# A two-layer hybrid decoder trunk on one core: side-by-side first tiles, sums of squares on VectorE, attention scores from split operands, and the scale of each norm taken up two or more tiles later

## The chip, the cores and the metric

The kernel runs on 1 core of a Trainium2 chip. The metric is the device time of one execution in microseconds (us), median of the runs. TensorE (PE in the rows) does the matmuls, VectorE (DVE) and ScalarE (ACT) the elementwise work, GpSimd (POOL) some of it, and the DMA queue of SyncE (SP) brings the weights.

## The reference

Two layers over a sequence of 256 positions with 2048 channels, all in float32. Cut to what matters:

```python
for l in range(2):
    h = rms_norm(x, attn_norm_g[l])        # x * rsqrt(mean(x*x) + 1e-6) * g
    proj = h @ w_in[l]                     # 2048 -> 11026 columns, split into the branches
    p_a = silu(layer_norm(causal_conv31(a_val * sigmoid(a_gate)))) @ w_conv_out[l]   # 512 channels
    p_b = (rg_lru(causal_conv4(r_x)) * gelu(r_gate)) @ w_rnn_out[l]                 # 768 channels
    p_c = nsa_attention(...) @ w_attn_out[l]     # 6 query heads, 2 key/value heads of 128
    y = sigmoid(g_a) * p_a + sigmoid(g_b) * p_b + sigmoid(g_c) * p_c
    x = x + y @ w_o[l]
    h2 = rms_norm(x, mlp_norm_g[l])
    x = x + square(relu(h2 @ w_mlp_up[l])) @ w_mlp_down[l]     # 2048 -> 8192 -> 2048
return rms_norm(x, final_norm_g)
```

With 256 positions the two softmax branches of the attention beside the compressed one ("selected" and "window") both see every earlier position, so each has plain causal scores, q times k, one 256 by 256 matrix for each head and branch.

## The kernel before

Activations lie transposed, channels on the partitions, so a product of 2048 channels with a block of 128 output columns is one **unit**: 16 **pairs** of matmuls into one PSUM tile `pu` (`unit2`, line 211). Each float32 operand is split into a high part (rounded to the fast float32r format) and a low remainder. A pair is `wh` times the 512 columns of an `xhl` tile (256 high, 256 low), then `wl` times its 256 high columns; the two halves of `pu` are added when it is read out (`z`, lines 674 and 675). Weights come in halves of a unit, 8 blocks of 128 by 128: `wload` (line 186) loads `raw` by SP's queue, ScalarE rounds it to `wh`, VectorE subtracts to `wl`. `wnext` keeps three halves ahead (`AHEAD`), with four buffers for each of the three tiles. Each `xhl` tile is made by ScalarE (high) and VectorE (low) in `scaled`.

The opening (lines 631 to 638) queues two 512-column parts of the first half, four transfers of `x` (two tiles of 256 each, 256 KB), two parts of the second half, and the other four of `x`. The first unit then uses the tiles one after another.

The factor of a norm is not applied to `x` but to each unit's result, as `z * rb`. `squares` (line 308) forms the squares of the 16 tiles on ScalarE, and GpSimd adds 14 of them into `ssq[0]`; the last stays apart. In layer 0 all the squares follow the opening. `rsqrt_cols` (line 325) then runs four one-column float32 matmuls (two tiles, two halves of the sequence) that sum over the partitions, VectorE adds the epsilon, GpSimd takes the power -1/2, and two float32 matmuls spread the result over 128 partitions into `rb`. It is called after the first unit of each normed stage (lines 672 and 748), and every result waits for `rb`.

Beside the units run side tasks written as generators: the convolution branch (`conv_task`), the recurrent one (`rnn_task`), and the attention (`attn_task`). `pump` (line 257) lets a task take its next steps after a half or a unit when an estimate of the engines' time allows, and `finish` forces the rest before the unit that needs its result. The order on each engine is then set by Tile's scheduler from a model of time; `keep` pins an instruction to the order in which it is written.

In `conv_task` the layer norm over the 512 channels uses four float32 matmuls with `mean_w` and, for the squares, eight one-column ones. In `attn_task` (lines 584 to 628) each of 6 heads has two score tiles, one for each half of the queries: one float32 matmul of `qr` with `kr` for both branches (line 593; 2 by 128 or 2 by 256 columns), then one bfloat16 matmul that adds the causal mask in PSUM (line 594, `identb` and `causb`), then VectorE takes the row maximum. So there are 24 score tiles in the two layers, 12 of each size.

In the trace one float32 matmul stands as two records, so 8 records are 4 matmuls.

## Time and profile before

| | us |
|---|---|
| median of 3 runs | 2869.32 (2869.1 to 2869.8) |
| the profiled execution | 2869.82 |
| its span in the profile | 2867.7 |
| TensorE busy | 2845.9 (99%) |
| VectorE busy | 2078.6 (72%) |
| ScalarE busy | 1469.7 (51%) |
| GpSimd busy | 108.2 (4%) |

Busy time of TensorE counts matmuls that overlap in its pipeline, so its pace is read from the starts of successive matmuls. The profiled execution took 2.1 us more than its span, for what lies around it.

### The profile page before, as it was taken

How to read it: one execution, taken by the hardware profiler on the slowest of the kernel's cores; microseconds unless marked ns; L12 is line 12 of the kernel's file. 1: busy time of each engine (PE TensorE's matmuls, PEld its weight loads, DVE VectorE, ACT ScalarE, POOL GpSimd, SP SyncE). 2: the span in 40 equal slices, each digit the busy share in tenths (PEclk: the TensorE clock that was granted, in tenths of full speed). 3: DMA queues.
4: the chain of work that ended last, by engine and by line, in shares of the span. 5: the costliest groups of instructions: out<-in, count | busy, mean ns of one | idle time of the engine just before them, and what ended most of it. 6: DMA issues, size and time to landing. Idle time of an engine off the chain costs nothing.

```text
span 2867.7 us, 43143 instructions
## 1 busy us (share of the span) xinstructions
PE 2845.9 (99%) x16456; PEld 2496.3 (87%) x16456; DVE 2078.6 (72%) x3332; ACT 1469.7 (51%) x2249; POOL 108.2 (4%) x102
## 2 busy tenths in 40 slices
PE   8999999999999999999999999999999999999998
PEld 6888888888888888888888888888888888888888
DVE  7988877677676576665779788776776766756655
ACT  5448755555444344443544487555554444434444
POOL 2000000002000000000200000000020000000001
PEclk9999999999999999999999999999999999999999
DMA  6555654565555555555555556445555555555554
GB/s 216 191 184 171 205 171 153 188 195 190 187 189 190 191 191 191 190 189 189 190 187 190 178 184 212 155 158 186 195 190 188 190 189 189 190 190 191 193 190 148
DMA packets 153167, 534.29 MB, mean 186 GB/s; under 512 B 17280, under 2 KB 18176, under 8 KB 152960
## 3 DMA queue, kind: packets, MB, share of 16 engines
q1 hardware_dynamic: 151904, 529.15, 55.7%
q8 instruction: 129, 2.11, 0.3%
q0 software_dynamic: 768, 2.13, 0.3%
q14 instruction: 78, 0.64, 0.1%
q10 hardware_dynamic: 288, 0.26, 0.0%
HBM read 529.37 MB, written 2.10 MB: 185 GB/s over the span
## 4 chain that ended last, share of the span: by engine, by line
PE 98%; DMA 0%; ACT 0%; POOL 0%; DVE 0%; SPq 0%; issue 0%; POOLq 0%; DVEq 0%; ACTq 0%
PE pu L155 95%; PE pv L155 3%; POOL ssq L317 0%; PE pv L614 0%; DMA x<-in_xT_dram 0%; DMA raw<-in_win_dram 0%; ACT wh L151 0%; ACT sq L151 0%; DVE fin L132 0%; PE pv L575 0%; PE pv L493 0%; SPq L637 0%; SPq L193 0%; POOLq L934 0%; DVEq L934 0%
## 5 line engine op out<-in xcount | busy, mean ns | idle before, releaser
L151 ACT ACTIVATE wh<-raw 128x1024 fp32r<-128x1024 f32 (+2 forms) x1034 | 1067.6, 1033 | 1305.9 <-PE pu L155 698.7
L155 PE MATMUL pu<-xhl,wh 128*128 128x512 f32 x4800 | 1681.1, 393 | 9.6 <-DVE xhl L136 9.6
L132 DVE TENSOR_TENSOR wl<-raw,wh 128x1024 fp32r<-128x1024 f32 (+2 forms) x1034 | 1230.8, 1191 | 628.0 <-ACT wh L151 604.3
L155 PE MATMUL pu<-xhl,wl 128*128 128x256 f32 x4800 | 1348.6, 281 | 1.2 <-DVE wl L132 1.2
L155 PEld LDWEIGHTS pu<-xhl,wh 128*128 128x128 f32 x4800 | 899.8, 187 | 209.2 <-DVE xhl L136 10.0
L155 PEld LDWEIGHTS pu<-xhl,wl 128*128 128x128 f32 x4800 | 908.4, 189 | 5.3 <-DVE wl L132 1.8
L155 PE MATMUL pu<-ah,wh 128*128 128x512 f32 x2016 | 699.1, 391 | 0.0
L155 PE MATMUL pu<-ah,wl 128*128 128x256 f32 x2016 | 564.5, 280 | 0.0
L155 PEld LDWEIGHTS pu<-ah,wh 128*128 128x128 f32 x2016 | 377.0, 187 | 82.7
L155 PEld LDWEIGHTS pu<-ah,wl 128*128 128x128 f32 x2016 | 381.0, 189 | 0.0
L132 DVE TENSOR_TENSOR x<-x,pu 128x256 f32<-128x256 f32 x316 | 132.7, 421 | 87.9 <-PE pu L155 82.6
L155 PE MATMUL pu<-yhl,wh 128*128 128x512 f32 x512 | 177.5, 393 | 0.0
L317 POOL TENSOR_TENSOR ssq<-ssq,sq 128x256 f32<-128x256 f32 x69 | 91.1, 1320 | 2239.1 <-ACT sq L151 2238.1
L155 PE MATMUL pu<-yhl,wl 128*128 128x256 f32 x512 | 141.7, 277 | 0.0
L155 PEld LDWEIGHTS pu<-yhl,wh 128*128 128x128 f32 x512 | 95.8, 187 | 22.0
L132 DVE TENSOR_TENSOR z<-pu,z 128x256 f32<-128x256 f32 x268 | 111.1, 416 | 0.6 <-ACT z L151 0.6
L136 DVE SCALAR_TENSOR_TENSOR cacc<-u,hpar,cacc 128x255 f32<-128x255 f32 (+14 forms) x240 | 103.7, 461 | 0.0
L151 ACT ACTIVATE z<-pu 128x256 f32<-128x256 f32 x268 | 97.9, 368 | 0.0
L155 PEld LDWEIGHTS pu<-yhl,wl 128*128 128x128 f32 x512 | 96.2, 188 | 0.2
L155 PE MATMUL pu<-oh,wh 128*128 128x512 f32 x192 | 67.4, 391 | 0.0
L132 DVE TENSOR_TENSOR z<-z,rb 128x256 f32<-128x256 f32 x136 | 57.7, 424 | 5.1 <-ACT rb L151 0.8
L136 DVE SCALAR_TENSOR_TENSOR s<-z 128x256 f32<-128x256 f32 x128 | 54.3, 425 | 4.5
(284 smaller groups left out, 1681.7 us busy)
## 6 DMA issues: line engine op xcount, KB each, us to landing
raw<-in_win_dram SPq DMA_DIRECT2D x342, 512.0 KB, 3.3
raw<-in_wup_dram SPq DMA_DIRECT2D x256, 512.0 KB, 3.5
raw<-in_wdn_dram SPq DMA_DIRECT2D x256, 512.0 KB, 4.2
raw<-in_wo_dram SPq DMA_DIRECT2D x64, 512.0 KB, 4.3
raw<-in_wro_dram SPq DMA_DIRECT2D x32, 384.0 KB, 3.0
raw<-in_wao_dram SPq DMA_DIRECT2D x32, 384.0 KB, 3.2
raw<-in_wco_dram SPq DMA_DIRECT2D x32, 256.0 KB, 2.9
raw<-in_cw_dram SPq DMA_DIRECT2D x16, 512.0 KB, 4.2
```

Source lines behind the costliest of these rows:

```text
L132: return V.tensor_tensor(o, x, y, op=op)
L136: return V.scalar_tensor_tensor(o, x, s, y, op0=op0, op1=op1)
L151: return A.activation(o, x, f, scale=scale, **kw)
L155: return T.matmul(o, l, r, start=start, stop=stop)
L317: G.tensor_tensor(ssq[0], ssq[0], q, op=ALU.add)
```

## The change

Four parts, and what goes with them.

1. The opening. Transfers of `x` and 512-column weight parts now alternate, and the parts alternate between the first and second unit. The matmuls of these two units run in turn, four tiles of `x` at a time (`early`, `tile2`). Ahead of them, 12 bfloat16 matmuls on a constant tile `wz` run whose result nobody reads.
2. The norms. In layer 0 the squares are formed beside units 2 and 3 as eight tiles of 512 columns, and VectorE adds them (`sq0`); for the other norms GpSimd still adds 14 tiles, and VectorE adds the last one. `rsqrt_cols` is cut in two: `rsqrt_rows` and `spread`. Each is placed between the `wh` and the `wl` matmul of a given tile, pinned there: in layer 0 the sums in unit 5 and the spreading in unit 6, elsewhere in units 1 and 2. Results before that are kept (`late`, `waiting`) and finished in one go.
3. The layer norm in `conv_task`: VectorE adds the four channel blocks first, so that one matmul with `mean_w` and two one-column matmuls remain.
4. The scores: `qr` and `kr` are split into high and low, three float32r matmuls (high with high, high with low, low with high) take the place of the one in float32, and VectorE adds the mask in PSUM. `identb` and `causb` are gone.

```diff
+    def tile2(p, w, i, r, k, n, between=None):
+        h, lo = (v[:, i * 128:(i + 1) * 128] for v in w)
+        r1 = mm(p, h, r.rearrange("p a s -> p (a s)"), k == 0, False)
+        if between:
+            keep(r1)
+            between()
+        r2 = mm(p[:, :S], lo, r[:, 0, :], False, k == n - 1)
+        if between:
+            keep(r2)
...
-        if m in (0, KT - 1):
-            ssq[m] = q
+        if m == 0:
+            ssq[0] = q
+        elif m == KT - 1:
+            tt(ssq[0], ssq[0], q, ALU.add)
...
-        for m in range(4):
-            mm(p[:, :S], mean_w, at[m], m == 0, m == 3, 4)
+        tt(cs, acc[0], acc[1], ALU.add)
+        tt(cs[:, 0, :], cs[:, 0, :], cs[:, 1, :], ALU.add)
+        mm(p[:, :S], mean_w, cs[:, 0, :], True, True, 4)
...
-        _, rb = rsqrt_cols([sq[m // 2][:, m % 2, :] for m in range(4)], 512)
+        tt(sq[0], sq[0], sq[1], ALU.add)
+        tt(sq[0][:, 0, :], sq[0][:, 0, :], sq[0][:, 1, :], ALU.add)
+        _, rb = rsqrt_cols([sq[0][:, 0, :]], 512)
...
-                    mm(pb[:, :, :nk], q, kr[:, g, :, :nk], True, False, 4)
-                    mm(pb[:, :, t * 128:nk], identb, causb, False, True)
+                    mm(pb[:, :, :nk], qh, krh[:, g, :, :nk], True, False)
+                    mm(pb[:, :, :nk], qh, krl[g][:, :, :nk], False, False)
+                    mm(pb[:, :, :nk], ql, krh[:, g, :, :nk], False, True)
+                    tt(pb[:, :, t * 128:nk], pb[:, :, t * 128:nk],
+                       con[:, None, C_CAUS:C_CAUS + 128].to_broadcast([128, 2, 128]), ALU.add)
...
+    for _ in range(N_WARM):
+        T.matmul(pz, wz[:, :128], wz, start=True, stop=True)
...
+    for i in range(8):
+        nc.sync.dma_start(x[:, 2 * i:2 * i + 2, :], a["xT"][:, 2 * i:2 * i + 2, :])
+        xs += [scaled(k, gain[:, 0, k:k + 1]) for k in (2 * i, 2 * i + 1)]
+        u, c = i % 2, i // 2
+        if c % 2 == 0:
+            wt[u] = wtiles()
+        wpart(wt[u], first[u + 2 * (c // 2)], slice(c % 2 * 512, c % 2 * 512 + 512))
+        if u:
+            for v in range(2):
+                for k in range(4 * c, 4 * c + 4):
+                    tile2(early[v], wt[v][1:], k % 8, xs[k], k, KT)
...
+        first_norm, rb_at = l == 0, RB_AT if l == 0 else 2
+        norm = {rb_at - 1: {4: norm_sums}, rb_at: {2: norm_spread}}
...
+            if l == 0 and ui in (2, 3):
+                for i in range(4 * ui - 8, 4 * ui - 4):
+                    keep(act(sq0[i], x[:, 2 * i:2 * i + 2, :], AF.Square))
+                    if i:
+                        keep(tt(sq0[0], sq0[0], sq0[i], ALU.add))
+            late.append((nm, m, z))
+            if ui < rb_at:
+                continue
```

(`RB_AT` is 6, `N_WARM` 12.) How this moves instructions, at three places. On TensorE at the opening, before: all pairs write the first unit's tile `pu_178`.

```order
L155 MATMUL pu_178<-xhl_114,wh_105 128x512
L155 MATMUL pu_178<-xhl_114,wl_106 128x256
L155 MATMUL pu_178<-xhl_117,wh_105 128x512
L155 MATMUL pu_178<-xhl_117,wl_106 128x256
L155 MATMUL pu_178<-xhl_121,wh_105 128x512
L155 MATMUL pu_178<-xhl_121,wl_106 128x256
```

And now, behind the last of the twelve on `wz`: `pu_117` and `pu_118` are the tiles of the first and second unit, and the numbers on `xhl` tell the tiles of `x` apart.

```order
L680 MATMUL pv_102<-wz_100 128x512
L157 MATMUL pu_117<-xhl_120,wh_127 128x512
L157 MATMUL pu_117<-xhl_120,wl_128 128x256
L157 MATMUL pu_117<-xhl_123,wh_127 128x512
L157 MATMUL pu_117<-xhl_123,wl_128 128x256
L157 MATMUL pu_117<-xhl_133,wh_127 128x512
L157 MATMUL pu_117<-xhl_133,wl_128 128x256
L157 MATMUL pu_118<-xhl_120,wh_140 128x512
L157 MATMUL pu_117<-xhl_136,wh_127 128x512
L157 MATMUL pu_117<-xhl_136,wl_128 128x256
L157 MATMUL pu_118<-xhl_120,wl_141 128x256
```

Each tile of `x` is now used twice before the ninth pair asks for the fifth one. On TensorE at the norm of layer 0, before: the sums over `ssq` and `sq` stand in the fourth unit (`pu_391`), after 58 pairs.

```order
L155 MATMUL pu_391<-xhl_154,wh_366 128x512
L155 MATMUL pu_391<-xhl_154,wl_367 128x256
L155 MATMUL pv_271<-ones_84,ssq_225 128x1
L155 MATMUL pv_271<-ones_84,sq_269 128x1
L155 MATMUL pv_271<-ones_84,ssq_225 128x1
L155 MATMUL pv_271<-ones_84,sq_269 128x1
L155 MATMUL pu_391<-xhl_158,wh_366 128x512
```

Now: they stand between the two passes of the fifth tile of the sixth unit (`pu_462`), after 88 pairs, and the scheduler has put the first passes of the seventh (`pu_519`) ahead of them.

```order
L157 MATMUL pu_462<-xhl_162,wh_416 128x512
L157 MATMUL pu_519<-xhl_120,wh_464 128x512
L157 MATMUL pu_519<-xhl_120,wl_465 128x256
L157 MATMUL pu_519<-xhl_123,wh_464 128x512
L157 MATMUL pu_519<-xhl_123,wl_465 128x256
L157 MATMUL pu_519<-xhl_133,wh_464 128x512
L157 MATMUL pv_478<-ones_84,sq0_295 128x1 x4
L157 MATMUL pu_462<-xhl_162,wl_417 128x256
```

The spreading matmuls follow 11 pairs later, where before they followed 15 pairs after the sums. On VectorE at one score tile of 2 by 256 columns in layer 0, before: `nm` is the row maximum of the tile `pv_4327`.

```order
L132 TENSOR_TENSOR wl_4497<-raw_4495,wh_4496 128x1024
L597 TENSOR_REDUCE nm_4330<-pv_4327 128x2
L132 TENSOR_TENSOR wl_4532<-raw_4530,wh_4531 128x1024
L132 TENSOR_TENSOR el_4253<-pv_4248,eh_4252 128x384
L132 TENSOR_TENSOR z_4477<-pu_4412,z_4477 128x256
```

Now: the mask is added to the tile `pv_4815` in place, and the subtraction of a weight half and a result `z` stand between it and the maximum.

```order
L143 TENSOR_SCALAR e_4652<-e_4652,rg_4650 128x128 x2
L134 TENSOR_TENSOR pv_4815<-pv_4815,con_81 128x2x128
L134 TENSOR_TENSOR wl_4867<-raw_4865,wh_4866 128x768
L134 TENSOR_TENSOR z_4803<-pu_4755,z_4803 128x256
L641 TENSOR_REDUCE nm_4820<-pv_4815 128x2
```

In layer 0 TensorE's last matmul of the attention stood 191 pairs ahead of the first unit that uses its result, and now stands 43 ahead; in layer 1 it was 191 and is 73. Between the third score tile of 2 by 256 columns of the first head group and the first transposition of its weights there were 18 pairs in either layer, and there are now 24 in layer 0 and 25 in layer 1.

## Rows read from the trace of the kernel before

**Rows 1.** The page's first part: busy time of each engine, its share of the span, and the count of instructions; PE and PEld (weight loads) first.

```profile
PE 2845.9 (99%) x16456; PEld 2496.3 (87%) x16456; DVE 2078.6 (72%) x3332; ACT 1469.7 (51%) x2249; POOL 108.2 (4%) x102
```

**Rows 2.** The view of waits, for TensorE: who waited for whom, us in total, times, the longest.

```profile
PE pu L155 <- DVE xhl L136: 9.6, 2, 8.7
PE pv L155 <- POOL ssq L317: 3.3, 1, 3.3
```

**Rows 3.** The view of instruction groups with shapes kept apart, TensorE, in the stretch from 100 to 200 us: count, busy us, mean ns of one, idle time before.

```profile
L155 PE MATMUL pu<-xhl,wh 128*128 128x512 f32 x290 | 100.6, 391 | 0.0
```

**Rows 4.** The opening. First the timeline of TensorE (start us, duration us), then its groups in the stretch from 8.74 to 30.11 us, then the timeline of ScalarE and of VectorE.

```profile
8.75 0.80 PE L155 MATMUL pu<-xhl,wh 128*128 128x512 f32 x1 [8.75 <-DVE xhl L136]
...
L155 PE MATMUL pu<-xhl,wh 128*128 128x512 f32 x48 | 18.8, 428 | 9.6 <-DVE xhl L136 9.6
...
4.50 1.26 ACT L151 ACTIVATE wh<-raw 128x512 fp32r<-128x512 f32 x2 [2.27 <-DMA raw<-in_win_dram]
7.67 1.71 ACT L151 ACTIVATE xhl<-x,gain 128x256 fp32r<-128x256 f32 x4 [1.91 <-DMA x<-in_xT_dram]
10.09 1.70 ACT L151 ACTIVATE xhl<-x,gain 128x256 fp32r<-128x256 f32 x4 [0.72 <-DMA x<-in_xT_dram]
11.70 1.13 ACT L151 ACTIVATE wh<-raw 128x512 fp32r<-128x512 f32 x2
12.77 3.31 ACT L151 ACTIVATE xhl<-x,gain 128x256 fp32r<-128x256 f32 x8
...
12.35 1.29 DVE L132 TENSOR_TENSOR wl<-raw,wh 128x512 fp32r<-128x512 f32 x2
13.56 3.25 DVE L136 SCALAR_TENSOR_TENSOR xhl<-x,gain,xhl 128x256 fp32r<-128x256 f32 x8
```

**Rows 5.** The first norm of layer 0. The timeline of TensorE; then the busy time of each engine (with counts), the granted clock (PEclk), the DMA share and GB/s in the stretch from 35.70 to 42.53 us; then TensorE's groups in the stretch from 30.17 to 48.74 us; then the timeline of GpSimd.

```profile
33.47 0.28 PE L155 MATMUL pu<-xhl,wl 128*128 128x256 f32 x1
37.09 0.58 PE L155 MATMUL pv<-ones,ssq 128*128 128x1 f32 x2 [3.34 <-POOL ssq L317]
...
39.60 0.63 PE L155 MATMUL pu<-xhl,wh 128*128 128x512 f32 x1
...
40.24 0.63 PE L155 MATMUL pu<-xhl,wh 128*128 128x512 f32 x1
...
35.70:42.53 6.83, 5.45 (x19) 4.92 (x20) 1.08 (x3) 0.00 (x0) 4.30 (x3) 0.50 0.54 172
...
L155 PE MATMUL pu<-xhl,wh 128*128 128x512 f32 x32 | 13.0, 441 | 0.0
...
19.07 17.97 POOL L317 TENSOR_TENSOR ssq<-ssq,sq 128x256 f32<-128x256 f32 x14 [17.90 <-ACT sq L151]
39.23 0.72 POOL L334 TENSOR_TENSOR rc<-rc,half 128x2 f32<-128x2 f32 x1 [2.19 <-DVE rc L142]
```

**Rows 6.** The timeline of TensorE at the second norm of layer 0.

```profile
732.48 0.28 PE L155 MATMUL pv<-ones,ssq 128*128 128x1 f32 x2
...
733.07 0.48 PE L155 MATMUL pu<-xhl,wh 128*128 128x512 f32 x1
...
733.50 0.28 PE L155 MATMUL pv<-ones,sq 128*128 128x1 f32 x2
733.64 0.48 PE L155 MATMUL pu<-xhl,wh 128*128 128x512 f32 x1
```

**Rows 7.** The timeline of TensorE at the layer norm of the convolution branch, layer 0.

```profile
201.28 1.89 PE L155 MATMUL pv<-cacc,mean_w 128*128 128x256 f32 x8
202.82 0.58 PE L155 MATMUL pu<-xhl,wh 128*128 128x512 f32 x1
...
207.86 0.50 PE L155 MATMUL pv<-ones,csq 128*128 128x1 f32 x4
208.22 0.48 PE L155 MATMUL pu<-xhl,wh 128*128 128x512 f32 x1
...
212.47 1.39 PE L155 MATMUL pv<-ones,csq 128*128 128x1 f32 x12
213.73 0.48 PE L155 MATMUL pu<-xhl,wh 128*128 128x512 f32 x1
```

**Rows 8.** The timeline of TensorE at a score tile of 2 by 128 columns, and at one of 2 by 256.

```profile
406.74 0.59 PE L155 MATMUL pv<-kr,qr 128*128 128x256 f32 x2
...
407.37 0.44 PE L155 MATMUL pv<-pcT,vcn 45*128 45x384 f32 x1
...
457.34 0.40 PE L155 MATMUL pu<-xhl,wh 128*128 128x512 f32 x1
457.57 0.28 PE L155 MATMUL pu<-xhl,wl 128*128 128x256 f32 x1
457.69 1.02 PE L155 MATMUL pv<-kr,qr 128*128 128x512 f32 x2
...
458.57 0.48 PE L155 MATMUL pu<-xhl,wh 128*128 128x512 f32 x1
```

**Rows 9.** The timeline of VectorE in the attention stretch, and the busy time of each engine from 390 to 495 us (columns as in rows 5).

```profile
401.55 0.42 DVE L132 TENSOR_TENSOR z<-pu,z 128x256 f32<-128x256 f32 x1
...
415.89 1.23 DVE L132 TENSOR_TENSOR wl<-raw,wh 128x1024 fp32r<-128x1024 f32 x1 [1.50 <-ACT wh L151]
...
390.00:495.00 105.00, 105.00 (x599) 88.46 (x598) 79.36 (x182) 60.29 (x144) 0.00 (x0) 1.00 0.44 141
```

More of the change, by code (lines that the diff above doesn't have):

```diff
@@ L498, in attn_task @@
             yield
-        kr = cpool.tile([128, NKV, 2, S], F32, tag="kr", name="kr")
+        krh = cpool.tile([128, NKV, 2, S], F32R, tag="kr", name="krh")
+        krl = [hl(F32R, "krl") for _ in range(NKV)]
         for b, nm in enumerate(("ks", "kw")):
-            swap_rope(kv[nm], kr[:, :, b, :])
+            r = hl(name="krf")
+            swap_rope(kv[nm], r)
+            act(krh[:, :, b, :], r, AF.Copy)
+            for g in range(NKV):
+                tt(krl[g][:, b, :], r[:, g, :], f32(krh[:, g, b, :]), ALU.subtract)
             yield
@@ L504, in attn_task @@
         for i in range(3):
-            r = hl(name="qr")
+            r = hl(name="qrf")
             swap_rope(qn[i], r)
-            qr.append(r)
+            q = [hl(F32R, "qr") for _ in range(2)]
+            act(q[0], r, AF.Copy)
+            tt(q[1], r, f32(q[0]), ALU.subtract)
+            qr.append(q)
             yield
@@ L646, in trunk, with norm_sums, norm_spread @@
         ct = rt = at_ = None
+        av, late = {}, []
+        def norm_sums():
+            nonlocal rc
+            rc = rsqrt_rows([sq0[0][:, 0, :], sq0[0][:, 1, :]] if first_norm else [ssq[0]], D, pin=True)
+        def norm_spread():
+            nonlocal rb
+            rb = spread(rc, pin=True)
+        first_norm, rb_at = l == 0, RB_AT if l == 0 else 2
+        norm = {rb_at - 1: {4: norm_sums}, rb_at: {2: norm_spread}}
         def pair(d, key, m, name):
@@ L724, in trunk @@
                     y["s", m] = r
+        for ui, (nm, m) in enumerate(PLAN):
+            task = dict(pa=ct, pb=rt, pc=at_).get(nm)
+            if task is not None and m == 0:
+                finish(task)
+            if nm in ("kc1", "vc1"):
+                compress(l, nm == "vc1", m, kv[nm[:2]], cz)
+                pump()
+                continue
+            if l == 0 and ui < 2:
+                p = early[ui]
+            else:
+                p = big_ps()
+                unit2(p, dict(pa=ua, pb=rbt, pc=oh).get(nm, xs), norm.get(ui))
+            z = tmp("z")
+            act(z, p[:, S:], AF.Copy)
+            tt(z, p[:, :S], z, ALU.add)
+            if l == 0 and ui in (2, 3):
[5 more added lines that the diff above has]
+            if ui < rb_at:
+                continue
+            if l == 0 and ui == rb_at:
+                side.append(prepare())
+            while late:
+                evict(*late.pop(0))
             pump()
```

139 lines of the change are left out of this document (69 added, 70 removed).

## The prediction

> **What bounds the kernel now.** I read the page's first part, then the waits of TensorE, then its timeline wherever something other than the main product stands. TensorE is busy 99% of the span, VectorE 72% [rows 1]. Busy time counts overlapping matmuls twice, so the pace is read from a stretch of main product alone: 290 first passes in 100 us with no idle time before any [rows 3], about 0.346 us a pair and 5.54 a unit. There the engine cannot be helped by anything that the change does. What can be won is therefore of two kinds: time in which TensorE stands or runs at its lower clock, and matmuls beside the main product. The list of waits is short: 9.6 us for the first `xhl` tiles and 3.3 for the sum of squares in the first norm [rows 2]. No wait in the attention reaches the list, so the work of the other engines counts only where it would come late.
>
> **The opening.** The first matmul starts at 8.75, and the third unit's last pair is the 48th first pass before 30.11 [rows 4]. At the full pace 48 pairs take 16.6 us, so 13.5 us of those 30.1 are start and stumbles. Now the same transfers of 256 KB come in another order on the same queue. The first arrives when the first did (4.50), the third at 7.67 and the fifth at 10.09, when ScalarE could begin on them [rows 4]; from then on ScalarE and VectorE, not the transfers, set the feed, since ScalarE worked through eight tiles in a row. One round (two tiles of `x`, one 512-column part) costs ScalarE 2 x 0.41 + 0.57 = 1.39 us and VectorE 2 x 0.41 + 0.65 = 1.46 [rows 4]. Six rounds are left when the fifth transfer lands, VectorE half a microsecond behind ScalarE: 10.5 + 6 x 1.46 = 19.3 for the last `wl` part. TensorE has 32 pairs, 11.1 us, for the two units; it starts near 6 (4.5, two tiles, one part) and is then fed 8 pairs (2.8 us) in every two rounds (2.9 us), so it keeps up, and after 19.3 it has the four last pairs of the second unit to do: 20.7. The next `wl` half is there by 19.3 + 1.23 [rows 9]. The third unit then ends at 20.7 + 5.5 = 26.2 against 30.1: **3.9 us won**. The transfers of the constants now stand among the weight halves of units 2 and 3; the second half of unit 2 is needed only 8 pairs, 2.8 us, after the first, so I cost that at nothing; without that cover it is one transfer, 0.7 us at the pace at which ScalarE took a round's two. The squares beside units 2 and 3 replace those that ScalarE did at the same place before. Bounds: were TensorE alone the limit from about 8.5 on (third transfer and two tiles), its remaining 30 pairs would end at 18.9, 5.7 us won. The other end is the lower clock all the way, below. I take 3.9, the feed by VectorE, since its rows are of the same instructions.
>
> The twelve matmuls on `wz` depend on nothing that comes by DMA and are over, even at 0.43 us each (a 512-column pass at the lower clock, which is two thirds of the 0.64 us from 39.60 to 40.24 [rows 5]), 5.2 us after they start, about when the first tiles come. They cost nothing, and whatever they win is inside the term above.
>
> **The first norm.** After 33.47 TensorE waits 3.34 us for `ssq`, because 14 additions on GpSimd run from 19.07 to 37.04 [rows 5]. Afterwards the granted clock is 0.50, the 1.2 GHz level, from 35.70 to 42.53, and a pair takes 0.64 us [rows 5]. The two units with 32 first passes, from 30.11 to 48.74, take 18.63 us where 32 x 0.346 = 11.07 would do; 7.56 us too many [rows 5]. What remains now: eight records of sums and four of spreading. Eight took 0.59 + 0.14 = 0.73 at the full clock [rows 6], and four small ones 0.36 [rows 7]. So 7.56 - 1.1 = **6.5 us won**, if no new wait comes. The new places: the squares of units 2 and 3 are done when unit 4 ends, near 37.3, and the sums stand after 88 pairs, which is 20.7 + 56 x 0.346 = 40.1. The power on GpSimd took 0.72 us and ended 1.3 us or so after the last sum [rows 5]; the spreading stands 11 pairs, 3.8 us, behind the sums. A margin of more than 2 us at either place. Behind VectorE's step for the epsilon stand a `wl` half and results, and TensorE waits for these only three halves later (8 us).
>
> **The other norms** (three) have four records of sums instead of eight: 0.73 to 0.36, **1.1 us** together. VectorE's one addition more is off the path: it waits for a GpSimd addition that follows a square by a microsecond or two, while the sums stand 20 pairs (7 us) later.
>
> **The layer norm of the convolution**, twice: eight records with `mean_w` take 202.82 - 201.28 = 1.54 us, now two, 0.39; and sixteen one-column records take 1.26 + 0.36, now four, 0.36 [rows 7]. (1.15 + 1.26) x 2 = **4.8 us**. The four extra additions on VectorE are side work of a task whose result is used several units later.
>
> **The scores.** A tile of 2 by 256 columns takes 458.57 - 457.69 = 0.88 us, mask included; three float32r passes of 512 columns at 0.23 (457.34 to 457.57) make 0.69 [rows 8]. 12 x 0.19 = 2.3. A tile of 2 by 128 columns takes 0.63 to the next start with the mask matmul at its full share [rows 8], or 0.44 as half of the larger tile; three passes of 256 columns at 0.12 (457.57 to 457.69) make 0.36. I take 0.53, the middle: 12 x 0.17 = 2.1, bounds 1.0 and 3.2. Together **4.4 us**, 3.3 to 5.5. VectorE gets 24 mask additions, of 256 columns from PSUM, about 0.42 us each by the `z` additions [rows 9], and the splitting of `qr` and `kr`, in a stretch in which it is busy 79.36 of 105 us [rows 9]. The mask addition waits for the third score matmul; queued behind it are a `wl` part and a `z`, as before behind the maximum. The `wl` part is used at least one unit later. I cost this at nothing, with what it would cost below.
>
> **Sum.** 3.9 + 6.5 + 1.1 + 4.8 + 4.4 = 20.7 us. The span was 2867.7, so 2847.0, and 2849.1 with the 2.1 us around it; the profiled execution was 0.5 us above the median, so I predict **2848.6 us**.
>
> **Rivals.**
>
> (a) *The opening runs at the lower clock.* TensorE now starts with a few pairs and waits for the third transfer, and in this trace the clock was at its lower level after a wait of 3.34 us [rows 5]. If all 32 pairs took 0.64 us from 6.0 on, they would end at 26.5 and the third unit at 32.0, 1.9 us later than before, so 2848.6 + 5.8 = 2854.4. Against it: at the lower clock the same feed keeps TensorE busy without a gap (eight pairs 5.1 us, fed every 2.9), and it was in such a busy stretch that the clock rose before. I give 9%.
> The Trainium skill (TensorE: Matmul & The Clock Gate, section HAM oscillation — how this bites in real kernels) speaks against such an opening: short groups of matmuls parted by waits for DMA let the clock fall, and each group starts slow. The row at 35.70 agrees for one wait; no run here shows it yet for a chain of groups.
>
> (b) *A wait in place of the one removed.* The seven results kept in layer 0 are finished at once in unit 6, some 6 us of VectorE work beside 2.5 us of `wl` per unit; or the squares are late. If TensorE stands at the spreading or for a `wl` as long as it did before, with the lower clock after it, the 6.5 us are gone: 2855.1. Against it are the margins above and the three halves in hand. 9%.
>
> (c) *Slower: the attention.* The mask addition lengthens the chain of each score tile on VectorE, and an addition that comes behind a `wl` half costs 0.42 + 1.23 us [rows 9]. If TensorE stood that long at the transpositions of all 24 tiles, 39.6 us would be added: about 2888. It decides against the change from (20.7 + 5.7) / 24 = 1.1 us a tile. Against it: the order leaves 24 and 25 pairs (8.3 us) between the last score tile of a row of heads and the first transposition, where 18 (6.2 us) were enough for no wait. For it: in layer 0 the whole task now ends 43 pairs, 15 us, ahead of its user instead of 66 us. 4%; a part of it, up to a loss of 15 us, another 5% (2856 to 2864).
>
> (d) The forecast itself, 73%, with 2845.7 (scores 5.5, opening 5.7) to 2852 (scores 3.3, opening 1.5) as its own range.
>
> **How the numbers follow.** The likeliest case gives 2848.6. The range takes in the forecast's own bounds, (a) and (b): 2845.5 to 2856; what is left out is (c) in both forms, 9%, and the tails of the others. About 0.2% (5.7 us) is what a measurement of this kernel can tell from no change. Cases (a), (b), (d) and half of the partial (c) all lie below 2863.6: faster 0.92, same 0.04, slower 0.04.
>
> **What would show it.** In the profile after: the 48th first pass ends near 26 us; no wait for `ssq` or `sq0`, and full clock from there to the end; a busy time of TensorE lower by some 10 to 14 us; 0.36 us for the sums of the later norms; three passes with no gap at each score tile. A clock of 0.50 in the first 27 us is (a); an idle time of TensorE before the spreading matmul or a `wl` in units 6 to 9 is (b); waits for `e` at the transpositions are (c). The prediction is wrong if the sums on TensorE shrink as said and the time doesn't.

## The result, and the profile after

The changed kernel takes 2850.15 us (median of 4 runs, 2849.82 to 2852.05), the kernel before on the same chip 2869.21 (4 runs, 2868.08 to 2869.8): a ratio of 0.9935, 95% interval 0.9918 to 0.9953, 19.1 us. The profiled execution took 2849.82 with a span of 2848.1, where before it was 2867.7. The forecast was 2848.6.

The page of the changed kernel, busy time of each engine, then the windows view from the first record of the clock to the end of TensorE's work (busy time of the engines, granted clock 1.00, DMA share, GB/s):

```profile
PE 2836.5 (100%) x16420; PEld 2490.8 (87%) x16420; DVE 2095.5 (74%) x3388; ACT 1473.7 (52%) x2253; POOL 91.1 (3%) x88
...
6.47:2842.90 2836.43, 2831.49 (x16409) 2488.84 (x16407) 2092.19 (x3383) 1470.15 (x2247) 90.51 (x80) 1.00 0.57 188
```

TensorE is busy 9.4 us less than in [rows 1], a little below the 10 to 14 us that the prediction gave as a sign; the twelve matmuls on `wz` are 5.2 us of what is new in it. The other 10.2 us of the span's gain are time in which TensorE stood. (Time at the lower clock counts as busy.) The view of waits, TensorE:

```profile
PE pv L157 <- POOL rc L902: 2.1, 1, 2.1
PE pv L680 <- DVE wz L677: 1.5, 1, 1.5
PE pv L157 <- DVE sq L134: 0.7, 1, 0.7
PE pu L157 <- DVE xhl L138: 0.5, 1, 0.5
PE pu L157 <- ACT wh L153: 0.4, 1, 0.4
PE pu L157 <- DVE wl L134: 0.2, 1, 0.2
```

The 9.6 and 3.3 us of [rows 2] are gone. The wait for `rc` belongs to the last norm and stood at 2.1 before too. The one for `sq` is new, 0.7 us, and none lies in the attention.

Where the time went is read by counting: TensorE's first passes of pairs (the `wh` matmuls into `pu`) are numbered in the order of their starts, and the same number is looked up in both traces. At the full pace a pair takes 0.3467 us, so a stretch's length says at once what it holds beyond the main product.

| stretch | before, us | after, us | won | forecast |
|---|---|---|---|---|
| start to pair 49 (three units) | 30.12 | 25.89 | 4.2 | 3.9 |
| pairs 49 to 113 (first norm) | 29.72 | 24.70 | 5.0 | 6.5 |
| the other three norms (their excess) | 4.31 | 2.75 | 1.6 | 1.1 |
| pairs 481 to 1393 (branches, layer 0) | 367.92 | 363.76 | 4.2 | 9.2 for |
| pairs 4400 to 5329 (branches, layer 1) | 373.83 | 368.73 | 5.1 | both layers |
| behind the last pair (from the first matmul of the last block to the end) | 20.63 | 21.02 | -0.4 | 0 |

The rows add up to 19.7, the difference of the spans.

**Opening.** TensorE's groups from 6.19 to 25.88 us, then its timeline at its start and at the first place where it stood (start us, duration us; the bracket is idle time before), then VectorE's timeline:

```profile
L157 PE MATMUL pu<-xhl,wh 128*128 128x512 f32 x48 | 17.3, 407 | 0.9 <-DVE xhl L138 0.5 <-ACT wh L153 0.4
```

```profile
1.46 5.22 PE L680 MATMUL pv<-wz 128*128 128x512 bf16 x12 [1.46 <-DVE wz L677]
6.20 0.72 PE L157 MATMUL pu<-xhl,wh 128*128 128x512 f32 x1
...
8.18 0.74 PE L157 MATMUL pu<-xhl,wh 128*128 128x512 f32 x2 [0.45 <-ACT wh L153]
...
9.12 0.39 PE L157 MATMUL pu<-xhl,wh 128*128 128x512 f32 x1
...
9.47 0.40 PE L157 MATMUL pu<-xhl,wh 128*128 128x512 f32 x1
```

```profile
17.80 0.69 DVE L134 TENSOR_TENSOR wl<-raw,wh 128x512 fp32r<-128x512 f32 x1
```

The 48th first pass lies before 25.88 where [rows 4] have it before 30.11. The last `wl` part is done at 18.49; the forecast had 19.3. After a wait of 0.45 us the pairs start 0.35 us apart (9.12, 9.47), the full pace. The end of the third unit is not exact to the tenth: in the nine traced executions with this opening (the changed kernel and eight of the runs below) it lies between 25.27 and 26.19.

**First norm.** TensorE at the sums (the product of `ones` with `sq`), then VectorE and ScalarE ahead of them, then the windows view around them (busy time of the engines, granted clock 1.00):

```profile
40.55 1.02 PE L157 MATMUL pv<-ones,sq 128*128 128x1 f32 x8 [0.66 <-DVE sq L134]
41.44 0.36 PE L157 MATMUL pu<-xhl,wl 128*128 128x256 f32 x1
```

```profile
38.59 1.22 DVE L134 TENSOR_TENSOR wl<-raw,wh 128x1024 fp32r<-128x1024 f32 x1 [0.74 <-ACT wh L153]
39.73 0.68 DVE L134 TENSOR_TENSOR sq<-sq,sq 128x512 f32<-128x512 f32 x1
```

```profile
37.49 1.06 ACT L153 ACTIVATE wh<-raw 128x1024 fp32r<-128x1024 f32 x1 [1.51 <-PE pu L157]
```

```profile
37.06:50.58 13.52, 12.86 (x79) 11.23 (x78) 8.39 (x15) 5.06 (x7) 0.71 (x1) 1.00 0.51 175
```

The last addition of squares stands in VectorE's queue behind a `wl` part, this waits for ScalarE's `wh`, and that waited 1.51 us for TensorE to free the buffer. So the addition comes 0.66 us late, with nothing wrong with the squares themselves. The clock holds, which it did not in [rows 5].

**Layer norm, a later norm, a score tile** of 2 by 256 columns, all in TensorE's timeline:

```profile
203.70 0.59 PE L157 MATMUL pv<-cs,mean_w 128*128 128x256 f32 x2
203.94 0.47 PE L157 MATMUL pu<-xhl,wl 128*128 128x256 f32 x1
...
216.27 0.50 PE L157 MATMUL pv<-ones,csq 128*128 128x1 f32 x4
216.63 0.37 PE L157 MATMUL pu<-xhl,wl 128*128 128x256 f32 x1
...
450.12 0.40 PE L157 MATMUL pv<-krh,qr 128*128 128x512 f32 x1
450.36 0.40 PE L157 MATMUL pv<-krl,qr 128*128 128x512 f32 x1
450.59 0.40 PE L157 MATMUL pv<-krh,qr 128*128 128x512 f32 x1
450.82 0.39 PE L157 MATMUL pu<-rb__2761,wh 128*128 128x512 f32 x1
...
721.05 0.50 PE L157 MATMUL pv<-ones,ssq 128*128 128x1 f32 x4
721.41 0.36 PE L157 MATMUL pu<-xhl,wl 128*128 128x256 f32 x1
```

The product with `mean_w` takes 0.24 us (1.54 in [rows 7]), the sums of `csq` 0.36 (1.62), a later norm's sums 0.36 (0.73 in [rows 6]), the score tile 0.70 without a gap (0.88 in [rows 8]).

### The profile page after: what moved, and what is told of

Its sections match the earlier page's. It is cut to its first block, busy times and chain, and to the rows that moved or that the text cites. A ratio compares the mean times of both kernels' runs of the same rounds, so it can differ in the third digit from the quotient of the medians.

```text
span 2848.1 us, 43089 instructions
## 1 busy us (share of the span) xinstructions
PE 2836.5 (100%) x16420; PEld 2490.8 (87%) x16420; DVE 2095.5 (74%) x3388; ACT 1473.7 (52%) x2253; POOL 91.1 (3%) x88
## 4 chain that ended last, share of the span: by engine, by line
PE 99%; DMA 0%; DVE 0%; ACT 0%; SPq 0%; issue 0%; POOLq 0%; DVEq 0%; ACTq 0%
PE pu L157 96%; PE pv L157 3%; PE pv L658 0%; DMA x<-in_xT_dram 0%; DMA raw<-in_win_dram 0%; DVE fin L134 0%; ACT wh L153 0%; PE pv L616 0%; DVE wl L134 0%; PE pv L526 0%; ACT xhl L153 0%; SPq L194 0%; SPq L688 0%; POOLq L1023 0%; DVE sq L134 0%
## 5 line engine op out<-in xcount | busy, mean ns | idle before, releaser
L331 POOL TENSOR_TENSOR ssq<-ssq,sq 128x256 f32<-128x256 f32 x55 | 73.8, 1342 | 2175.3 <-ACT sq L153 2170.7
```

The lines of the kernel that those rows point to most:

```text
L331: G.tensor_tensor(ssq[0], ssq[0], q, op=ALU.add)
```

## The experiments

Each kernel is the changed one with one edit. A median is compared with the kernel before on the same chip, by its ratio; where a stretch is compared with the changed kernel, it is by the pair numbers above.

**A second pace.** One thing has to be known to read them. TensorE's groups from 100 to 200 us, first in the changed kernel, then in the one without the matmuls on `wz` (below):

```profile
L157 PE MATMUL pu<-xhl,wh 128*128 128x512 f32 x290 | 100.6, 391 | 0.0
```

```profile
L157 PE MATMUL pu<-xhl,wh 128*128 128x512 f32 x284 | 100.4, 399 | 0.0
```

The instructions are the same, the granted clock is 1.00 in both, and neither waits, yet one starts 290 pairs and the other 284: 0.3467 and 0.3535 us a pair. Such a state lasts for tens to hundreds of pairs (last section). In pairs 113 to 721 it is there in some runs and not in others whose instructions are the same. It is called the longer pace below. In a stretch of main product alone that the edit doesn't touch it is told apart by its place. In the branches it is counted over the pairs that have no other matmul and no wait in them or just ahead: what these take beyond 0.3467 us each is longer pace, and the rest is other matmuls and waits.

### The opening

*Without the matmuls on `wz`* (e1_nowarm).

```diff
-N_WARM, RB_AT = 12, 6
+N_WARM, RB_AT = 0, 6
```

> The changed kernel without the twelve matmuls on the constant tile. Theory A (the opening is fed by VectorE, so the clock in its first part hardly matters): the first pairs take 0.64 us instead of 0.35, eight or so of them before the clock rises, TensorE catches up with the feed, and the third unit ends at most 1 us later than in the changed kernel (25.9 us): span 2848.1 to 2849.1. Rival (short groups of matmuls parted by waits keep the clock at its lower level through the opening): 32 pairs at 0.64 us, third unit's end near 31 to 32, span 2853 to 2854.

Measured 2852.19 (2851.57 to 2853.47), ratio 0.9944 [0.9932, 0.9957], span 2850.4. TensorE's timeline at the start:

```profile
10.57 0.63 PE L157 MATMUL pu<-xhl,wh 128*128 128x512 f32 x1
...
11.21 0.63 PE L157 MATMUL pu<-xhl,wh 128*128 128x512 f32 x1
...
12.36 0.40 PE L157 MATMUL pu<-xhl,wh 128*128 128x512 f32 x1
...
12.71 0.40 PE L157 MATMUL pu<-xhl,wh 128*128 128x512 f32 x1
```

Until about 12 us the pairs start 0.64 apart, as at the lower clock of [rows 5], then 0.35. Still the third unit ends at 26.30, 0.4 later than in the changed kernel and 0.1 outside the 25.27 to 26.19 of the executions with the warm-up, so a price of the missing warm-up is hardly clear of their spread. The feed sets that end, not TensorE, as the prediction argued against rival (a). The rest of the span's difference is not the opening: pairs 49 to 113 are 1.0 shorter (no wait for `sq`), and pairs 113 to 721 ran at the longer pace, 2.9 more.

*The old order of transfers, units one after the other, `wz` kept* (e6_seq_open).

```diff
-    for i in range(8):
-        nc.sync.dma_start(x[:, 2 * i:2 * i + 2, :], a["xT"][:, 2 * i:2 * i + 2, :])
...
-        wpart(wt[u], first[u + 2 * (c // 2)], slice(c % 2 * 512, c % 2 * 512 + 512))
...
+    for i in range(4):
...
+            for j in range(2):
+                wpart(wt[u], first[2 * u], slice(j * 512, j * 512 + 512))
+        for j in (2 * i, 2 * i + 1):
+            nc.sync.dma_start(x[:, 2 * j:2 * j + 2, :], a["xT"][:, 2 * j:2 * j + 2, :])
...
+    for v in range(2):
...
+        for k in range(KT):
+            tile2(early[v], wt[k // 8][1:], k % 8, xs[k], k, KT)
```

> The changed kernel with the opening's order of before (first unit's first half, four transfers of x, its second half, the rest of x; the two units one after the other), with the twelve matmuls on the constant tile and all else as changed. Theory A (the interleaving is worth what the feed allows): first pair at 8.7 at the full clock, the first unit follows the tiles of x to about 17.5, the second waits for its weights, the third ends near 29.5 instead of 25.9: 3.6 us more, span about 2851.7. Rival (the squares that no longer stand beside the opening were the gain): the third unit ends near 27, span below 2849.5.

Measured 2851.49 (2850.85 to 2854.8), ratio 0.9941 [0.9928, 0.9955], span 2849.0. The first pair starts at 8.38 and the third unit ends at 28.09, 2.2 later. TensorE stood 1.9 us between the last `wz` matmul and the first pair, and the clock fell in spite of the warm-up. TensorE's timeline, and the windows view from 9.54 to 12.95 (granted clock 0.50):

```profile
8.38 0.50 PE L157 MATMUL pu<-xhl,wh 128*128 128x512 f32 x1 [1.87 <-DVE xhl L138]
```

```profile
9.54:12.95 3.41, 3.41 (x13) 2.73 (x11) 3.38 (x8) 3.41 (x9) 0.00 (x0) 0.50 1.06 405
```

Pairs 49 to 113 are 1.1 shorter (no wait for `sq`, and a better pace), so that only 1.0 is left at the end.

*All squares straight behind the opening, summed on VectorE* (e11_sq_open): the loop moves ahead of the three `wload`s behind the opening. This is not quite the place of before: there ScalarE formed two weight halves first (16.05 and 17.32 us) and the squares from 18.28, and GpSimd added them, while here VectorE has the additions too.

```diff
+    for i in range(8):
+        keep(act(sq0[i], x[:, 2 * i:2 * i + 2, :], AF.Square))
+        if i:
+            keep(tt(sq0[0], sq0[0], sq0[i], ALU.add))
...
-            if l == 0 and ui in (2, 3):
-                for i in range(4 * ui - 8, 4 * ui - 4):
-                    keep(act(sq0[i], x[:, 2 * i:2 * i + 2, :], AF.Square))
-                    if i:
-                        keep(tt(sq0[0], sq0[0], sq0[i], ALU.add))
```

> The changed kernel with all squares of the first norm formed directly behind the opening's tiles, ahead of the first weight half of unit 2 (about where they stood before the change), added by VectorE. Theory A (where the squares stood was a part of the 4.2 us won at the opening, since ScalarE and VectorE feed TensorE there): the weights of unit 2 come some 4 us later, TensorE waits about 3 us near 20 us, the third unit ends near 29 instead of 25.9, perhaps with a piece at the lower clock behind it, and no wait is left at the sums: span 2850.5 to 2852.5. Rival (the interleaving alone made the opening): span below 2849.

Measured 2855.02 (2854.33 to 2855.73), ratio 0.9952 [0.9938, 0.9965], span 2853.9. The third unit ends at 32.51, 6.6 us later, twice what was expected. TensorE's timeline, and the windows view from 22.91 to 29.74:

```profile
23.22 0.80 PE L157 MATMUL pu<-xhl,wh 128*128 128x512 f32 x1 [2.66 <-ACT wh L153]
```

```profile
22.91:29.74 6.83, 5.54 (x16) 4.36 (x17) 6.60 (x9) 3.63 (x6) 0.00 (x0) 0.50 0.45 137
```

`wh` comes late behind the squares, TensorE stands 2.66 us, and the clock is 0.50 for the next 6.8. So squares and their additions ahead of the weights of the third unit cost the opening more than the order of transfers (2.2). How much of that the kernel before paid is not shown, since its squares stood two weight halves later and its additions on GpSimd.

### The first norm

*The sums one unit earlier* (e4_rb5).

```diff
-N_WARM, RB_AT = 12, 6
+N_WARM, RB_AT = 12, 5
```

> The changed kernel with the sums of the first norm one unit earlier (RB_AT 5 for 6). In VectorE's order the four last additions of squares then stand together, with no weight part among them. Theory A (what is late at the sums is a place in VectorE's queue): the squares of unit 3 end 35 us from the start, the last addition near 35.8, the sums are reached near 33.9, so TensorE waits about 1.9 us instead of 0.7: span 2849.0 to 2849.6, clock at its full level or briefly below it. Rival (the additions are done when they are, at 40.5, and the place of the sums in TensorE's order decides): a wait of 6 us or more and the lower clock after it, span 2854 to 2857.

Measured 2855.08 (2853.57 to 2857.21), ratio 0.9955 [0.9941, 0.9968], span 2852.4. TensorE and VectorE:

```profile
37.53 1.02 PE L157 MATMUL pv<-ones,sq 128*128 128x1 f32 x8 [3.12 <-DVE sq L134]
```

```profile
30.35 3.71 DVE L134 TENSOR_TENSOR wl<-raw,wh 128x1024 fp32r<-128x1024 f32 x3
...
34.31 3.07 DVE L134 TENSOR_TENSOR sq<-sq,sq 128x512 f32<-128x512 f32 x4
```

A wait of 3.1 with the clock at 0.50 from 39.63 to 43.05; pairs 49 to 113 take 3.9 us more. The additions are late because three `wl` parts stand ahead of them. The wait was larger than the 1.9 expected and less than the rival's 6; the place in the queue decides it.

*The sums two units later* (e2_rb8).

```diff
-N_WARM, RB_AT = 12, 6
+N_WARM, RB_AT = 12, 8
```

> The changed kernel with the sums of the first norm two units later (RB_AT 8 for 6). Theory A (the 0.7 us for which TensorE still waits at these sums is the lateness of VectorE's last addition, which stands behind a weight part whose buffer TensorE itself frees late): the wait is gone, nothing else becomes late, span 2847.3 to 2847.6. Rival (nine results finished at once instead of seven make VectorE late with weight parts in units 8 to 11): TensorE waits there for 1 us or more, span 2848.5 or longer.

Measured 2858.86 (2855.21 to 2859.53), ratio 0.9964 [0.9951, 0.9976], span 2857.0. At the norm it is as expected: no wait for `sq`. Pairs 49 to 113 are 2.1 us shorter and pairs 113 to 481 1.5 longer, for the sums and the spreading (1.35) now stand behind pair 113; together 0.6 is won, about the wait. But the span is 8.9 us longer, and pairs 721 to 1633 alone account for 9.8. TensorE's timeline there, and the windows behind the waits:

```profile
436.95 0.55 PE L157 MATMUL pu<-xhl,wh 128*128 128x512 f32 x1 [1.73 <-DVE z L134]
...
553.94 0.51 PE L157 MATMUL pu<-oh,wh 128*128 128x512 f32 x1 [0.69 <-DVE oh L134]
...
559.31 0.50 PE L157 MATMUL pu<-oh,wh 128*128 128x512 f32 x1 [1.92 <-DVE z L134]
```

```profile
437.21:440.62 3.41, 3.41 (x12) 2.85 (x12) 3.38 (x13) 0.42 (x1) 0.00 (x0) 0.50 0.04 12
560.09:563.50 3.41, 3.41 (x13) 2.93 (x12) 3.41 (x9) 1.08 (x3) 0.00 (x0) 0.50 0.80 250
```

Results that are kept for longer let the side tasks begin later, and the attention of layer 0, which the prediction had 43 pairs ahead of its user, now ends behind it: `oh` is the attention's output, and TensorE waits for it at the product that uses it. The first of the three waits is at another place: at 436.95 TensorE waits for a result `z` that VectorE read out behind steps of the attention's compressed branch. So a delay made at 50 us is paid at 437 and, for the larger part, at 550.

*The squares earlier: six beside unit 2, two beside unit 3* (e10_sq62).

```diff
-                for i in range(4 * ui - 8, 4 * ui - 4):
+                for i in range(0, 6) if ui == 2 else range(6, 8):
```

> The changed kernel with six of the eight square tiles of the first norm formed beside unit 2 and two beside unit 3 (four and four in the changed one). In VectorE's order the last addition then stands one weight part further ahead. Theory A (the 0.7 us of wait at the sums is that place in VectorE's queue): the last addition ends near 38 us, TensorE reaches the sums at 39.8 and doesn't wait; span 2847.2 to 2847.6, everything else as it was. Rival (more squares beside unit 2 make the weights of unit 3 late): a wait at 26 us of 1 us or more, span 2848.5 or longer.

Measured 2851.65 (2848.79 to 2851.93, 5 runs), ratio 0.9936 [0.9922, 0.9949], span 2849.9. The wait for `sq` is gone, and pairs 49 to 113 are 0.85 shorter: that much the wait cost, with its surroundings. (The third unit ends at 25.62, inside the spread named above.) But pairs 113 to 721 ran at the longer pace in this execution (2.9 more). Two of its five runs lie at 2848.79 and 2849.54; it is not shown to beat the changed kernel.

### The layer norm and the scores

*The sums of the layer norm on TensorE again* (e5_ln_pe).

```diff
-        tt(cs, acc[0], acc[1], ALU.add)
-        tt(cs[:, 0, :], cs[:, 0, :], cs[:, 1, :], ALU.add)
-        mm(p[:, :S], mean_w, cs[:, 0, :], True, True, 4)
+        for m in range(4):
+            mm(p[:, :S], mean_w, at[m], m == 0, m == 3, 4)
...
-        _, rb = rsqrt_cols([sq[0][:, 0, :]], 512)
+        _, rb = rsqrt_cols([sq[m // 2][:, m % 2, :] for m in range(4)], 512)
```

> The changed kernel with the layer norm of the convolution summed on TensorE again (four float32 matmuls with the mean and eight one-column ones, in each layer). Theory A (what the change won there is the time of these matmuls and nothing else): 1.54 and 1.62 us a layer instead of 0.25 and 0.36, so 2 x 2.55 = 5.1 us more, span about 2853.0, give or take 1 us for the pace of the pairs (0.347 or 0.354 us). Rival (VectorE's four additions cost TensorE time elsewhere, so undoing them gives part back): less than 3.5 us more.

Measured 2855.79 (2855.58 to 2858.14), ratio 0.9957 [0.9942, 0.9972], span 2853.8. Pairs 481 to 1393 take 2.05 more and 4400 to 5329 2.14: 4.2 us, where the forecast's term was 4.8. But these stretches have 1.1 us less of the longer pace than in the changed kernel (2.9 against 4.0); the matmuls and what surrounds them are 5.3 more, which is what theory A expected for the groups alone (5.1). So VectorE's four additions cost TensorE nothing elsewhere. The other 1.6 of the span is longer pace in layer 1's second half.

*Scores in one float32 product, mask on VectorE* (e3_fp32_scores).

```diff
-                    mm(pb[:, :, :nk], qh, krh[:, g, :, :nk], True, False)
-                    mm(pb[:, :, :nk], qh, krl[g][:, :, :nk], False, False)
-                    mm(pb[:, :, :nk], ql, krh[:, g, :, :nk], False, True)
+                    mm(pb[:, :, :nk], q, kr[:, g, :, :nk], True, True, 4)
```

(Cut: `qr` and `kr` are no longer split into high and low.)

> The changed kernel with the scores as one float32 matmul of unsplit operands again, mask still added by VectorE. Theory A (the scores were won on TensorE alone): a tile of 2 by 256 columns goes from 0.69 back to about 0.86 us, one of 2 by 128 from 0.35 to 0.43 to 0.5, so 12 x 0.17 + 12 x 0.1 = 3.2 us more, span 2850.8 to 2852. Rival (the mask matmul was the larger part of what the scores won): less than 1.5 us more, span below 2849.6.

Measured 2852.14 (2851.94 to 2852.21), ratio 0.9943 [0.9931, 0.9956], span 2850.4. The two branch stretches take 0.7 and 1.4 more, 2.1 us. Here too 0.8 us less of it is longer pace (3.2 against 4.0), so the split by itself is worth 3.0.

This trace also shows a wait in the opening, which the edit doesn't touch, that left the clock at its full level; TensorE:

```profile
9.29 0.73 PE L157 MATMUL pu<-xhl,wh 128*128 128x512 f32 x2 [1.73 <-ACT wh L153]
...
10.24 0.39 PE L157 MATMUL pu<-xhl,wh 128*128 128x512 f32 x1
...
10.59 0.40 PE L157 MATMUL pu<-xhl,wh 128*128 128x512 f32 x1
```

*Split scores, mask on TensorE* (e7_mask_pe).

```diff
-                    tt(pb[:, :, t * 128:nk], pb[:, :, t * 128:nk],
-                       con[:, None, C_CAUS:C_CAUS + 128].to_broadcast([128, 2, 128]), ALU.add)
+                    mm(pb[:, :, t * 128:nk], identb, causb, False, True)
```

(Cut: `identb` and `causb` are made again, and the third score matmul no longer ends the sum.)

> The changed kernel with the causal mask added by TensorE again (the bfloat16 matmul on the identity), scores split as changed. Theory A (that matmul hides almost wholly behind its neighbours: with unsplit scores and VectorE's mask, layer 1's stretch of attention took 43.26 us beyond the main product, with TensorE's mask and unsplit scores 43.44): 24 x 0.01 to 0.04 us, span 2848.2 to 2849.2. Rival (it costs its 256 columns, 0.11 us each): 2.6 us more, span 2850.7.

Measured 2854.37 (2852.56 to 2855.86), ratio 0.9949 [0.9935, 0.9962], span 2854.1. TensorE's timeline at a tile:

```profile
450.65 0.28 PE L157 MATMUL pv<-causb,identb 128*128 128x256 bf16 x1
450.68 0.36 PE L157 MATMUL pu<-xhl,wl 128*128 128x256 f32 x1
450.89 0.40 PE L157 MATMUL pu<-xhl,wh 128*128 128x512 f32 x1
```

From the mask to the next `wh` are 0.24 us, where a `wl` pass alone takes 0.12: the mask costs 0.12 here, though the `wl` pass starts only 0.03 behind it. By stretches it is 1.58 in pairs 721 to 1393 and 1.47 in 4400 to 5329, 3.05 us for 24 tiles, and the longer pace is the same there to 0.1; the other 2.9 of the span is longer pace in pairs 113 to 721. The theory that the bfloat16 matmul hides behind its neighbours fell. It rested on the 0.02 between its start and the next in [rows 8], and the row behind those shows what that left out; the kernel before, TensorE:

```profile
458.89 0.28 PE L155 MATMUL pu<-xhl,wl 128*128 128x256 f32 x1
```

The `wh` pass behind the tile is followed after 0.32 us, not after 0.23: the mask's price stands in the pass behind it. Counted to the second start behind the group, less one pass of that kind, the 2 by 256 tile takes 0.975 us before, 0.857 with float32 and no mask (e3_fp32_scores), 0.691 in the changed kernel and 0.823 here. So the mask is 0.12 to 0.13 with either product, and the split 0.15 to 0.17.

### How much room the attention has

*The mask added twice, and four times, on VectorE* (e8_mask2, e8_mask4; the masked weights are the same).

```diff
+                    for _ in range(2):          (e8_mask4: range(4))
                         tt(pb[:, :, t * 128:nk], pb[:, :, t * 128:nk],
```

> The changed kernel with the mask added twice: 24 more additions of 0.42 us on VectorE. The attention ends 3 pairs ahead of its user in layer 0 (1389 against 1392) and 34 ahead in layer 1. Theory B (it costs nothing until its end passes its user): span 2847.5 to 2850, no wait in layer 1; in layer 0, where only a microsecond is in hand, a wait of up to 2 us at the first of those units. Rival (c): waits at the transpositions, 0.4 us or more for each tile, 10 us.

Measured 2852.16 (2851.57 to 2852.39), ratio 0.9941 [0.9928, 0.9955], span 2850.5. The attention's stretches stand within 0.1 of the changed kernel's; the 2.5 of span are longer pace in pairs 1633 to 4400 (1.6) and a later end (0.9).

> The changed kernel with the mask added four times on VectorE for every score tile (the sum beyond the first changes no weight, as masked scores are already at -1e30): 24 x 3 more additions of 256 columns, some 30 us of VectorE. In the order the attention then ends 25 pairs behind the start of the units that use it in layer 0 and 25 behind in layer 1 (1417 against 1392, 5353 against 5328). Theory B (the side chain costs TensorE nothing until its end passes its user, then it costs about what the run with RB_AT 8 lost there): some 5 to 10 us at units 87 to 102 in each layer, no waits before; span 2858 to 2868. Rival (c) of the prediction (TensorE stands at the transpositions of each tile): waits at all 24 tiles, 24 x 1 us or more. Third view (VectorE has room, so nothing happens): span 2847.5 to 2849.

Measured 2862.56 (2860.34 to 2864.83), ratio 0.9978 [0.9969, 0.9987], span 2861.7. TensorE's timeline in layer 0, and the window behind the last wait:

```profile
548.18 0.44 PE L157 MATMUL pv<-eh,vn 128*128 128x384 f32 x1 [0.36 <-ACT eh L153]
...
557.70 0.79 PE L157 MATMUL pu<-oh,wh 128*128 128x512 f32 x1 [1.93 <-DVE z L134]
```

```profile
557.72:561.13 3.41, 3.41 (x11) 2.93 (x12) 3.41 (x7) 1.10 (x3) 0.00 (x0) 0.50 0.70 186
```

Pairs 721 to 1633 take 5.8 more, and layer 1's branch and what follows it 6.3 (pairs 4400 to the last, 1.8 of it longer pace). The rest of the span's 13.6 is longer pace in pairs 1633 to 4400 (1.6). No tile waits, except for the very last `eh` and `el`; the loss is at the user of `oh`. So one mask addition a tile is free, one more is free, and three more cost some 12 us (10 without the longer pace). The place at which it decides is the end of the whole task, not the tile.

*The sums two units later, and the side tasks let in more readily* (e9_rb8_slack12).

```diff
-N_WARM, RB_AT = 12, 6
+N_WARM, RB_AT = 12, 8
...
-AHEAD, SLACK, PE_SIDE = 3, 1.4, 0.4
+AHEAD, SLACK, PE_SIDE = 3, 1.2, 0.4
```

`SLACK` multiplies the time that `pump` counts for a side step on VectorE and ScalarE.

> The sums of the first norm two units later (RB_AT 8) as in the run that lost 9 us, and the planner's allowance for side work cut from 1.4 to 1.2 (SLACK), so that the attention of layer 0 ends 132 pairs ahead of the first unit that uses it instead of 25 behind it. Theory A (that run lost its time because the side tasks, started two units later, reached the user of the attention too late): no wait at units 27 to 87, the wait of 0.7 us at the sums gone as well, span 2847.2 to 2848. Rival (nine results finished at once, or the sums' place, make VectorE late whatever the allowance): span 2853 or more.

Measured 2856.74 (2855.95 to 2857.64), ratio 0.9957 [0.9945, 0.997], span 2853.8. The attention's loss is gone (no wait at the user of `oh`, pairs 1393 to 1633 as in the changed kernel, 721 to 1633 within 0.1), which bears out that lateness was the cause in e2_rb8. But crowded side work now makes TensorE wait elsewhere, once where the results of units beside the convolution branch are read out:

```profile
279.98 0.47 PE L157 MATMUL pu<-xhl,wh 128*128 128x512 f32 x1 [1.89 <-DVE z L134]
```

Pairs 481 to 721 take 1.8 more and 4400 to 5329 3.5 more; 0.9 of the latter, and the 1.7 behind pair 5329, are longer pace.

## Why the prediction was right, step by step

The sum held: 20.7 us forecast, 19.6 found in the span, and each term has a measured counterpart of the kind that was forecast. That the sum came so near is in part luck: the layer norm and the scores won some 2 us more than their terms, and the longer pace, of which the prediction knew nothing, took about as much back.

- **Opening, 3.9: measured 4.2.** The reason was right: the feed by ScalarE and VectorE sets the end. But the new order of transfers is only half of it: undone alone it costs 2.2, and with the old order the third unit still ends 2.0 before the 30.1 of [rows 4]. What is left of the changed opening in that run is above all the warm-up and the squares, which stand further back and are added on VectorE. The prediction costed the squares at nothing, as the same work at the same place; that their place matters is shown by the run that put them behind the opening (6.6), but not how much of the 2.0 is theirs. The warm-up, costed inside the term, is worth about 0.4 by the one run without it, hardly more than the spread.
- **Rival (a)** did not come. With gaps of 0.45 and 0.50 us the pace stays at 0.35 a pair, and without the warm-up the pairs do start at the lower pace, but the feed hides most of it. The Trainium skill (TensorE: Matmul & The Clock Gate, section HAM oscillation — how this bites in real kernels) has short groups parted by waits each start slow. The changed kernel's opening does not show it; the run with the old order (1.9 us of standing) and the one with the squares at the opening (2.66) show the slow start behind one wait each, and the run with float32 scores shows full pace behind one of 1.73. None shows a chain of slow groups.
- **First norm, 6.5: measured 5.0.** This term was too large. The sums and the spreading were right in kind, and the clock held. But the prediction took the last square as the end of that chain and gave it more than 2 us of margin; it left out that the last addition has its place in VectorE's queue behind a `wl` part whose own input is late. That costs 0.66 of wait, 0.85 with its surroundings, by e10_sq62. The eight sum records took 0.89 from start to next start (40.55 to 41.44) where 0.73 was taken, and a part of the units ran at the longer pace (0.2). Rival (b) was the right mechanism at a tenth of its price.
- **Other norms, 1.1: measured 1.6.** Counted to the second start behind each group, the sums go from 0.89 to 0.45, 1.3 for the three; the forecast took 0.73 to 0.36 and left out the stretched passes. The last 0.2 is longer pace in the kernel before.
- **Layer norm 4.8 and scores 4.4, together 9.2: measured 9.3.** This agreement is luck. Without the longer pace the two branch stretches are 11.05 shorter than before; the longer pace costs 4.0 us in them now and cost 2.2 before, which leaves 9.3. Undone one at a time, and again without the longer pace, the terms are 5.3 for the layer norm, 3.0 for the split and 3.15 for the mask, 11.4 together. So the scores are worth 6.1, outside the 3.3 to 5.5 that the prediction gave them. The cause is the same in both terms: the groups of before were measured to the next start, which left out what the pass behind each group is stretched (0.09 us for a mask or one-column sums, 0.19 for `mean_w`). Counted to the second start, the layer norm's groups go from 1.73 to 0.43 and from 1.79 to 0.45 in each layer, 5.3 in all, and a 2 by 256 score tile from 0.975 to 0.691, where the forecast had 0.88 to 0.69. Whether the shorter groups themselves bring on the longer pace was not tested.
- **Costed at nothing:** the mask additions and the additions of the layer norm on VectorE. For the mask that held, with one whole addition a tile to spare; for the layer norm's additions too, since the run that undid them gave back the price of the matmuls and no more. **Rival (c)** gave the right lever and the wrong place: TensorE would not have stood at the transpositions of 24 tiles, but at the user of the attention, and the point from which it decides lies between 24 and 72 further additions a kernel, as the two runs show.

## What to carry to other kernels

A step that is moved on an in-order engine arrives when its queue lets it, so its lateness is counted from what stands ahead of it there, not from its own input. Side work that is given a later start cost little here until its last step passed its user, and then it cost far from where the edit was made, so look for the margin at the user. The price of a small group of matmuls is read to the second start behind it, since the pass that follows may be the one that pays.

## What the hardware showed that was not expected

**Two paces at one granted clock.** The main product runs at 0.3467 or 0.3535 us a pair, with nothing waited for and the granted clock at 1.00. For pairs 113 to 481 the first was seen in the kernel before, the changed one, and in the runs with old order, earlier sums, squares at the opening, float32 scores, the old layer norm, and the mask added two or four times; the second in the ones without warm-up, with the mask on TensorE, and with six squares beside unit 2 (130.0 against 127.6 us each). (In both runs with later sums the same pairs take 129.05, but 1.35 of that is the sums and the spreading, which stand there.) In those three runs the state lasts from pair 100, just behind the spreading, to pair 546, where the first `mean_w` product stands. In the branches behind pair 721 it takes the same places in every run whose order there is that of the changed kernel, and others where an edit moved the matmuls. Counted in groups of four pairs, the changed kernel has 131 at the longer pace and the kernel before 69, which is 62 x 4 x 0.0068 = 1.7 us, nearly all of it in the branches; the spread of runs of one kernel by 2 to 2.5 us (2849.8 and 2852.05) would fit it too, but that is only argued: those runs have no trace. What enters or ends the state is open.

**The clock after short waits.** It fell to 0.50 after waits of 1.73 (436.95 us in e2_rb8), 1.87, 1.92, 1.93, 2.66, 3.12 and, in the kernel before, 3.34 us, and held after one of 1.73 (9.29 us in e3_fp32_scores), one of 1.89 (279.98 us in e9_rb8_slack12) and after those of 0.4 to 1.1. The two of 1.73 went either way, so the length of the wait alone does not decide it. In e1_nowarm the column of the granted clock reads 1.00 also in the first 12 us, where the pairs start 0.64 apart, so there the starts are the evidence.

**A pass pays for the group ahead of it.** The main product's first pass behind one-column sums or the mask is followed 0.09 us later than otherwise, and the one behind `mean_w` 0.19 later; behind a score tile split into float32r passes there is no such time (0.693 to the next start, 0.691 by the full count).
